# Spreading the inverse norms of the differential heads: transposes on TensorE or two transfers through DRAM

## The chip, the cores and the metric

The kernel runs on one core of one Trainium2 chip. A core has five engines with instruction queues of their own: TensorE (PE; its weight loads are listed as PEld), VectorE (DVE), ScalarE (ACT), GpSimd (POOL) and SyncE (SP), which here only issues transfers. Each engine works through its queue in order, and waits at an instruction until the semaphores that it names are reached. 16 DMA engines carry out the transfers. Matmul results go to PSUM banks; everything else lies in SBUF, 128 partitions wide, or in DRAM.

The metric is device time of one execution in microseconds (us). Before the change it was 1777.44 us, the median of three runs from 1776.35 to 1777.76.

## The reference

Two layers over 512 tokens of width 1024. Each layer mixes tokens in three branches (differential attention, a convolution module, neighbourhood attention), merges them by gates, and goes on to a feed-forward block and a gated embedding. What concerns this change is the end of the differential attention:

```python
def diff_attention(qa, ka, va, lq1, lk1, lq2, lk2, subln_g, lam_init, cos, sin):
    ...
    def block(qi):
        s = jnp.einsum('bhcqd,bhckd->bhcqk', qi, k).astype(f32) * scale
        a = jax.nn.softmax(s, axis=-1)
        a = (a[:, :, 0] - lam * a[:, :, 1]).astype(v.dtype)
        return jnp.einsum('bhqk,bhkd->bhqd', a, v)
    o = lax.map(block, qb)
    o = o.transpose(1, 2, 0, 3, 4).reshape(B, HA, S, DV_A)
    o = rmsnorm(o, subln_g) * (1.0 - lam_init)
    return o.transpose(0, 2, 1, 3).reshape(B, S, WIDTH_A)
```

There are four heads of 128 value channels. For each head and token the norm needs one number, the inverse root of the mean square over the 128 channels.

## The kernel before

**Layout.** Activations stand with channels on partitions and the 512 tokens along the free dimension, so a head's output `o` is one tile of 128 x 512. Its norm sums over partitions. All products are done in three passes on split operands (`split`, line 162: ACT makes the high part, DVE subtracts it for the low part; `mm3`, line 175: three matmuls). Weights come by SP into three raw buffers `wr` (`weights`, line 166), are split into three buffers `wh` and `wl`, and are used by TensorE some tiles later. When a raw buffer is split, the next load may go into it.

**Order.** The order on TensorE is written by hand. Work that runs beside the projections is a generator: after every four chunks of three matmuls `tick` (line 94) advances the generators whose delay has run out; a `yield n` puts the next part n ticks later. For the other engines a scheduler places instructions by priority and by what they need; `behind` (line 1064) adds that one instruction may not go before another, without a wait. On SP the order of transfers is fixed in the same way, and a transfer that waits holds all that stand behind it.

**The head's norm.** `diff_unit` (line 844) makes scores and probabilities of a quarter of the queries (`probs`, line 892), transposes the probabilities and multiplies them by the values. When a head's output is complete in the bank `av`, ACT writes its squares to `sq` (tag `ss`, one buffer) and a scaled copy to `o` (tag `t`). Then `norm` (line 206) runs:

1. After 1 tick, four transposes of `sq` into a PSUM bank `tr` (line 213), tokens now on partitions.
2. DVE sums over the free dimension and adds epsilon (lines 216 to 221), which gives `ms`, 128 x 4: token 128c + p in row p, column c.
3. POOL raises it to the power -0.5, which gives the column `col` (tag `rc`, line 223).
4. After 2 ticks, four more transposes (line 227). Each takes one column of `col`, repeated 128 times, and so puts the inverse norms of 128 tokens as a row on all 128 partitions. They fill a bank `bc` of 128 x 512.
5. `done` (line 884): DVE multiplies `o` by `bc`, read from PSUM, ACT and DVE split it into a tile `y`, which the merge of the branches (`merge_a`, line 776) multiplies much later.

`norm` has other users too (the norms over the model width, the convolution's norm). They pass `spread=True` and copy `bc` to SBUF first. Only the differential heads pass `spread=False`.

While the heads' norms run, TensorE goes on with projections: the third and fourth heads' query and key (`diff_in`, line 813), the gates (`gate_c`, `gate_b`), the product of the third branch (`branch_c`, line 769). `diff_in` sends four copies of 32 rows over SP for each rotation (`diff_rp`, line 829) and stacks the halves by more copies (line 660). DVE fills its time with taps of the convolution (`conv_z`).

Of the kernel before, what the change touches and what calls it, by code (L numbers as in the profile page):

```python
# [11 lines left out]
F32 = mybir.dt.float32  # L12
# [3 lines left out]
ALU = mybir.AluOpType  # L16
# [4 lines left out]
P = 128  # L21
L = 2
S = 512
# [4 lines left out]
HA = 4  # L28
# [33 lines left out]
class Net:  # L62
# [143 lines left out]
    def norm(self, sq, n, waits, done, spread=True, eps=None):  # L206


        nc = self.nc
        yield waits[0]  # L210
        st = self.ps("tr", (P, 4, P))
        for c in range(4):
            nc.tensor.transpose(st[:, c, :], sq[:, c * P:(c + 1) * P], self.ident)
        with self.tc.high_priority(offset=min(200, self.tc.cur_priority - self.p0) if n == D and self.p0 is not None else 0):
            sm = self.sb("sm", [P, 4])
            nc.vector.tensor_reduce(out=sm, in_=st, op=ALU.add, axis=AX.X)
            ms = self.sb("sm", [P, 4])
            if eps is None:
                nc.vector.tensor_scalar(ms, sm, 1.0 / n, EPS, ALU.mult, ALU.add)
            else:  # L220
                self.stt(ms, sm, 1.0 / n, eps, ALU.mult, ALU.add)
            col = self.sb("rc", [P, 4])
            nc.gpsimd.tensor_tensor(col, ms, self.power, ALU.pow)
        yield waits[1]
        bc = self.ps("tr", (P, 4, P))
        for c in range(4):
            nc.tensor.transpose(bc[:, c, :], col[:, c:c + 1].to_broadcast([P, P]), self.ident)
        bc = bc.rearrange("p a b -> p (a b)")
        done(col, self.spread(bc) if spread else bc)

    def rows(self, col, rb):
        self.col, self.rb = col, rb
# [59 lines left out]
    def build(self):  # L292
        nc, tc, a = self.nc, self.tc, self.a
        self.bufs = dict(wr=3, wh=3, wl=3, h=8, qk=2, kh=2, v=4, pt=2, y=5, z=5, x=4, t=7, rp=4,
                         e=4, a=3, r=2, rb=1, ss=1, sm=8, rc=4, b=2, s=8)
        self.bg, self.w_ahead = BG, 400
        self.pbufs = dict(mm=3, sc=2, tr=2, av=1)
        with tc.tile_pool(name="sb", bufs=1) as self.pool, \
                tc.tile_pool(name="ps", bufs=1, space=PSUM) as self.psum, \
                tc.tile_pool(name="dr", bufs=1, space=DRAM) as dram:  # L300
            xs = dram.tile([KD, P, 512], F32, name="xs")
            self.pis = dram.tile([KD, P, 512], F32, name="pis")
            with tc.manual_schedule(engines={mybir.EngineType.PE}):
                h = self.opening()
                xsrc = a["xT"]
                for i in range(L):
                    h = self.layer(i, h, xsrc, xs)
                    xsrc = xs
# [535 lines left out]
    def diff_unit(self, head, qt, st4, k2, st, box, ys):  # L844

        nc, i = self.nc, self.i
        half, t = qt // 2, qt % 2
        box[qt] = self.probs(st4, k2, qt, box["s0"])
        if t == 0:
            return  # L850
        yield 3
        ats = [box[2 * half], box[2 * half + 1]]
        pps = []
        for kp in range(2):
            pt = self.ps("tr", (P, 2, 256))
            for u in range(2):
                for t in range(2):
                    kc = 2 * kp + u
                    nc.tensor.transpose(pt[:, u, t * P:(t + 1) * P],
                                        ats[t][:, kc * P:(kc + 1) * P], self.ident)  # L860
            pp = self.sb("pt", [P, 2, 2, 256], F32R)
            self.split(pp[:, 0], pp[:, 1], pt)
            pps.append(pp)
        yield 2
        if half == 0:
            box["av"] = self.ps("av")
        av = box["av"]
        cs = slice((head % 2) * P, (head % 2) * P + P)
        for kp in range(2):
            for u in range(2):  # L870
                v = st["v", head // 2][kp][:, u].rearrange("p (a b) -> p a b", a=2)
                self.mm3(av[:, half * 256:half * 256 + 256], v[:, 0, cs], v[:, 1, cs],
                         pps[kp][:, 0, u], pps[kp][:, 1, u], kp * 2 + u == 0, kp * 2 + u == 3)
        if half == 0:
            return

        eps = self.sb("sm", [P, 4])
        self.stt(eps, box["s0"], EPS, box["s0"], ALU.mult, ALU.mult)
        o = self.sb("t", [P, 512])
        sq = self.sb("ss", [P, 512])  # L880
        self.act(sq, av, AF.Square)
        self.act(o, av, AF.Copy, scale=self.subg[:, i:i + 1])

        def done(col, bc):
            self.tt(o, o, bc, ALU.mult)
            y = self.sb("y", [P, 2, 512], F32R)
            self.split(y[:, 0, :], y[:, 1, :], o)
            ys.append(y)

        yield from self.norm(sq, P, (1, 2), done, spread=False, eps=eps)  # L890

    def probs(self, st4, k2, qt, s0):


        nc, i = self.nc, self.i
        qs = slice(qt * P, (qt + 1) * P)
        m = self.sb("s", [P, 10])
        es = []
        for u in range(2):
            sc = self.ps("sc")  # L900
            self.scores(sc, st4, k2, u, qs, slice(0, 512))
            nc.vector.tensor_reduce(out=m[:, u:u + 1], in_=sc, op=ALU.max, axis=AX.X, negate=True)  # L902
            e = self.sb("e" if u else "a", [P, 512])
            self.act(e, sc, AF.Exp, table="exp", bias=m[:, u:u + 1],
                     accum_out=m[:, 3:4] if u else s0[:, qt:qt + 1])
            es.append(e)
        nc.vector.reciprocal(m[:, 4:5], m[:, 3:4])
        self.stt(m[:, 5:6], m[:, 4:5], self.nlam[:, i:i + 1], s0[:, qt:qt + 1],
                 ALU.mult, ALU.mult)
        self.stt(es[0], es[1], m[:, 5:6], es[0], ALU.mult, ALU.add)  # L910
        return es[0]

    def w_o(self, mg, xsrc):
# [553 lines left out]
```

## Time and profile before

| | us |
|---|---|
| median of three runs | 1777.44 |
| lowest and highest run | 1776.35, 1777.76 |
| profiled execution, first to last instruction (its span) | 1776.7 |
| DVE busy in the span | 1421.7 |
| line 227, differential heads: 32 transposes, length of one | 0.272 |
| line 213, differential heads: 32 transposes, length of one | 0.272 |
| line 223, differential heads: 8 powers on POOL, length of one | 1.0 to 1.5 |

For the profiled execution only the span is listed. Its matmuls overlap: the next starts before the last has ended, so what a matmul costs is read from the distance of starts, not from its length. A row of the timeline gives start, length, engine, line, operation, tiles written and read, shape, and in brackets the idle time of the engine before it with what ended it. Line 157 and 160 are helpers of DVE, line 143 one of ACT; such rows are told apart by their tiles. SPq is SP's queue: the length of its row is the time from one transfer's start of issue to the end of issue, waits between merged ones included.

### The profile page before, as it was taken

What the parts mean: (1) busy time and instruction counts of PE and PEld (TensorE: products, weight loads), DVE (VectorE), ACT (ScalarE), POOL (GpSimd) and SP (SyncE); (2) the same over time, 40 slices, a digit from 0 to 9 for tenths busy, and PEclk for the clock granted to TensorE, in tenths of its full rate; (3) what the DMA queues carried; (4) which work ended last, traced back from release to release, by engine and by line L of the source; (5) the groups of instructions that cost most, each with busy time, mean ns of one, the idle gap of its engine ahead of it and who ended that gap; (6) DMA issues with size and microseconds to landing.
All of it is one profiled execution on the core that took longest, in us unless ns stands there. A gap on an engine that the chain in (4) does not pass through costs nothing.

```text
span 1776.7 us, 27451 instructions
## 1 busy us (share of the span) xinstructions
PE 1767.5 (99%) x10210; PEld 1559.6 (88%) x10210; DVE 1421.7 (80%) x2418; ACT 894.4 (50%) x1561; POOL 103.0 (6%) x146
## 2 busy tenths in 40 slices
PE   9999999999999999999999999999999999999998
PEld 7888888888899899998888888888888998989987
DVE  7878887998798587787776788889887976867776
ACT  5577555225565254454545765452356643534454
POOL 0000000000111010100000000000001110101000
PEclk9999999999999999999999999999999999999999
DMA  5666641334757366543447655423357664655332
GB/s 202 188 186 176 161 125 42 113 98 140 230 150 193 109 167 160 132 131 123 145 124 198 176 165 149 113 71 95 93 179 198 171 179 115 173 144 151 98 108 92
DMA packets 113509, 256.07 MB, mean 144 GB/s; under 512 B 14560, under 2 KB 19424, under 8 KB 113376
## 3 DMA queue, kind: packets, MB, share of 16 engines
q1 hardware_dynamic: 99984, 229.93, 42.3%
q0 software_dynamic: 12672, 23.07, 8.3%
q8 instruction: 81, 1.33, 0.3%
q10 hardware_dynamic: 720, 1.31, 0.2%
q14 instruction: 52, 0.43, 0.1%
HBM read 215.46 MB, written 7.34 MB: 125 GB/s over the span
## 4 chain that ended last, share of the span: by engine, by line
PE 96%; DVE 2%; ACT 1%; issue 0%; DMA 0%; POOL 0%; ACTq 0%; POOLq 0%; DVEq 0%
PE ffn_mm L1017 4%; PE ffn_mm L1019 4%; PE ffn_mm L177 4%; PE ffn_mm L179 4%; PE ffn_mm L178 4%; PE ffn_mm L1018 4%; PE ffn_sc L1019 3%; PE ffn_sc L1017 3%; PE ffn_sc L1018 3%; PE mergea_mm L177 2%; PE mergea_mm L178 2%; PE mergea_mm L179 2%; PE diff_sc L811 2%; PE gatec_mm L177 2%; PE gatec_mm L178 2%; PE gatec_mm L179 2%
## 5 line engine op out<-in xcount | busy, mean ns | idle before, releaser
L160 DVE SCALAR_TENSOR_TENSOR conv_z<-glu_z,pre_par,conv_z 128x512 f32<-128x512 f32 x240 | 179.4, 748 | 3.3
L143 ACT ACTIVATE ffn_wh<-ffn_wr 128x1024 fp32r<-128x1024 f32 (+1 forms) x92 | 92.7, 1014 | 111.7 <-PE ffn_mm L178 77.1
L987 POOL DMA_DIRECT2D ffn_qk<-w_fu x88 | 78.0, 990 | 605.7 <-DMA ffn_qk<-w_fu 414.7
L157 DVE TENSOR_TENSOR ffn_wl<-ffn_wr,ffn_wh 128x1024 fp32r<-128x1024 f32 (+1 forms) x92 | 107.4, 1173 | 5.4 <-ACT ffn_wh L143 4.9
L157 DVE TENSOR_TENSOR ffn_t<-ffn_mm,wo_rb 128x512 f32<-128x512 f32 (+1 forms) x64 | 38.6, 604 | 67.9 <-PE ffn_mm L179 67.8
L143 ACT ACTIVATE mergea_wh<-mergea_wr 128x1024 fp32r<-128x1024 f32 (+1 forms) x32 | 27.1, 846 | 96.8 <-PE mergea_mm L178 79.6
L143 ACT ACTIVATE ffn_wh<-ffn_qk 128x1024 fp32r<-128x1024 f32 x44 | 46.7, 1060 | 35.9 <-PE ffn_mm L178 15.7
L157 DVE TENSOR_TENSOR ffn_wl<-ffn_qk,ffn_wh 128x1024 fp32r<-128x1024 f32 x44 | 53.8, 1224 | 11.3 <-ACT ffn_wh L143 11.3
L157 DVE TENSOR_TENSOR ffn_t<-ffn_t,ffn_t 128x512 f32<-128x512 f32 (+1 forms) x46 | 31.3, 680 | 31.4 <-ACT ffn_t L143 30.9
L143 ACT ACTIVATE diff_a<-diff_sc,diff_s 128x512 f32<-128x512 f32 x32 | 22.0, 686 | 61.0 <-DVE diff_s L902 61.0
L177 PE MATMUL ffn_mm<-ffn_v,ffn_wh 128*128 128x512 f32 x132 | 51.4, 389 | 0.0
L178 PE MATMUL ffn_mm<-ffn_v,ffn_wh 128*128 128x512 f32 x132 | 51.4, 389 | 0.0
L179 PE MATMUL ffn_mm<-ffn_v,ffn_wl 128*128 128x512 f32 x132 | 51.3, 389 | 0.0
L177 PE MATMUL ffn_mm<-ffn_y,ffn_wh 128*128 128x512 f32 x132 | 51.3, 389 | 0.0
L178 PE MATMUL ffn_mm<-ffn_y,ffn_wh 128*128 128x512 f32 x132 | 51.3, 389 | 0.0
L179 PE MATMUL ffn_mm<-ffn_y,ffn_wl 128*128 128x512 f32 x132 | 51.3, 389 | 0.0
L1019 PE MATMUL ffn_mm<-wo_h,ffn_wl 128*128 128x256 f32 x176 | 49.8, 283 | 0.0
L1019 PE MATMUL ffn_sc<-wo_h,ffn_wl 128*128 128x256 f32 x176 | 49.8, 283 | 0.0
L1018 PE MATMUL ffn_mm<-wo_h,ffn_wh 128*128 128x256 f32 x176 | 49.8, 283 | 0.0
L1018 PE MATMUL ffn_sc<-wo_h,ffn_wh 128*128 128x256 f32 x176 | 49.8, 283 | 0.0
L1017 PE MATMUL ffn_sc<-wo_h,ffn_wh 128*128 128x256 f32 x176 | 49.8, 283 | 0.0
L1017 PE MATMUL ffn_mm<-wo_h,ffn_wh 128*128 128x256 f32 x176 | 49.8, 283 | 0.0
(876 smaller groups left out, 6588.6 us busy)
## 6 DMA issues: line engine op xcount, KB each, us to landing
ffn_qk<-w_fu POOLq DMA_DIRECT2D x88, 256.0 KB, 5.7
ffn_wr<-w_fg SPq DMA_DIRECT2D x44, 512.0 KB, 3.7
ffn_wr<-w_fd SPq DMA_DIRECT2D x32, 448.0 KB, 3.9
ffn_r<-w_fu SPq DMA_DIRECT2D x44, 256.0 KB, 3.7
ffn_qk<-w_fg SPq DMA_DIRECT2D x44, 256.0 KB, 4.3
ffn_qk<-w_fu SPq DMA_DIRECT2D x44, 256.0 KB, 4.6
natten_wr<-w_in SPq DMA_DIRECT2D x16, 512.0 KB, 4.3
natten_b<-bias SPq DMA_DIRECT2D x32, 256.0 KB, 4.0
```

The source lines that it names most:

```text
L143: i = self.nc.scalar.activation(out, in_, func, **kw)
L157: return self.nc.vector.tensor_tensor(out, a, b, op)
L160: return self.nc.vector.scalar_tensor_tensor(out, a, s, b, op0, op1)
L177: mm(out, wh, ah, start=first, stop=False)
L178: mm(out, wh, al, start=False, stop=False)
L179: mm(out, wl, ah, start=False, stop=last)
L811: self.nc.tensor.matmul(out, st4[:, u, qs], st[:, ks], start=n == 0, stop=n == 1)
L987: nc.gpsimd.dma_start(q, wu[:, lo], accum_op=ALU.add)
L1017: mm(out, wh[:, c], bh, start=first and k == 0, stop=False, skip_group_check=True)
L1018: mm(out, wh[:, c], bl, start=False, stop=False, skip_group_check=True)
L1019: mm(out, wl[:, c], bh, start=False, stop=k == 3, skip_group_check=True)
```

## The change

For the differential heads the second four transposes are gone. SP writes the 128 x 4 column to a row of 512 numbers in DRAM, element by element, and reads this row back on all 128 partitions, into the buffer of the squares. The multiplication reads SBUF where it read PSUM; it is placed four ticks after the statistics, where it was two, and it may go ahead neither of the latest weight split nor of the latest part of the probabilities.

```diff
@@ norm
             col = self.sb("rc", [P, 4])
             nc.gpsimd.tensor_tensor(col, ms, self.power, ALU.pow)
+        if not spread:
+            rows, self.rowed = self.nrm[self.rowed], self.rowed + 1
+            with nc.allow_non_contiguous_dma(reason="column to row"):
+                nc.sync.dma_start(rows.rearrange("(c p) -> p c", p=P), col)
+            nc.sync.dma_start(sq, rows[None, :].to_broadcast([P, S]))
+            yield sum(waits[1:])
+            return done(col, sq)
         yield waits[1]
...
-        done(col, self.spread(bc) if spread else bc)
+        done(col, self.spread(bc))
@@ build
+            self.nrm, self.rowed = dram.tile([L * HA, S], F32, name="nrm"), 0
@@ diff_unit
-            self.split(pp[:, 0], pp[:, 1], pt)
+            self.prob = self.split(pp[:, 0], pp[:, 1], pt)
...
         def done(col, bc):
-            self.tt(o, o, bc, ALU.mult)
+            i = self.tt(o, o, bc, ALU.mult)
+            self.behind(i, self.low)
+            self.behind(i, self.prob)
...
-        yield from self.norm(sq, P, (1, 2), done, spread=False, eps=eps)
+        yield from self.norm(sq, P, (1, 4), done, spread=False, eps=eps)
@@ probs
-        self.stt(es[0], es[1], m[:, 5:6], es[0], ALU.mult, ALU.add)
+        self.prob = self.stt(es[0], es[1], m[:, 5:6], es[0], ALU.mult, ALU.add)
```

In the changed program TensorE has the same order without the eight groups of four transposes, and POOL's order is unchanged. On SP the two transfers of head 0 stand between two loads of weights for the gates; those of head 1 before a load for the second gates; those of head 2 after the third load of the third branch's weights; those of head 3 around the last load for the second gates, the write before it and the read after it. On DVE the multiplication of heads 0, 1 and 2 stands right behind the mix of the next probabilities, that of head 3 between the low parts of the last two gate weights; some taps of the convolution and the splits of the head outputs have moved. On ACT the load of the sigmoid table and two of its uses stand a little earlier.

## The prediction

> **What bounds the kernel now.** I began with the page: span, busy shares, and the chain of work that ended last.
>
> ```profile
> span 1776.7 us, 27451 instructions
> PE 1767.5 (99%) x10210; PEld 1559.6 (88%) x10210; DVE 1421.7 (80%) x2418; ACT 894.4 (50%) x1561; POOL 103.0 (6%) x146
> PE 96%; DVE 2%; ACT 1%; issue 0%; DMA 0%; POOL 0%; ACTq 0%; POOLq 0%; DVEq 0%
> ```
>
> TensorE carries 96% of the chain. A busy share of 99% is not proof, since matmul records overlap, so next came the view of waits for PE alone (waits, times, longest) and the busy time by stretch in the stage that the change touches (differential heads, layer 0).
>
> ```profile
> PE pre_av L325 <- DVE pre_zeror L398: 1.1, 1, 1.1
> PE natten_tr L734 <- ACT natten_e L143: 0.3, 2, 0.2
> PE natten_tr L736 <- ACT natten_e L143: 0.3, 2, 0.2
> PE natten_tr L736 <- DVE natten_a L157: 0.2, 1, 0.2
> ...
> 217.00:320.00 103.00, 103.00 (x529) 86.99 (x528) 85.88 (x148) 52.74 (x103) 4.53 (x4) 1.00 0.34 97
> ```
>
> All waits of PE add up to 1.9 us, and none is in the touched stage, where PE is busy for 103.00 of 103.00 us at full granted clock. DVE is next with 85.88 us; the DMA engines are at 0.34. So here a TensorE instruction removed is time removed, and an instruction of another engine costs only when it is late enough to stop TensorE.
>
> The Trainium skill ("Perfetto Trace Analysis", section Identifying the Most-Contended Engine) says that matmul busy time measures headroom badly, because matmuls are pipelined, and that the busy share of weight loads is better. By that rule PE is 88% and not 99% full here, and removed PE work might win nothing; this is rival C, and the starts of the matmuls below decide it.
>
> **The price of the removed transposes.** The line's own group, then PE in order of time (start, length) around head 0, and further down a place with the same neighbours and no transposes.
>
> ```profile
> L227 PE MATMUL diff_tr<-pre_ident,diff_rc x32: 270/272/273, 224.9 to 1194.4; 128*128 128x128 f32 x32
> ...
> 224.65 0.39 PE L179 MATMUL diff_mm<-glu_h,diff_wl 128*128 128x512 f32 x1
> 224.88 0.60 PE L227 MATMUL diff_tr<-pre_ident,diff_rc 128*128 128x128 f32 x4
> 225.23 0.47 PE L811 MATMUL diff_sc<-diff_qk 128*128 128x512 f32 x1
> ...
> 226.24 0.39 PE L177 MATMUL diff_mm<-glu_h,diff_wh 128*128 128x512 f32 x1
> ...
> 227.85 0.39 PE L178 MATMUL diff_mm<-glu_h,diff_wh 128*128 128x512 f32 x1
> ...
> 232.94 0.39 PE L179 MATMUL gatec_mm<-glu_h,gatec_wl 128*128 128x512 f32 x1
> ...
> 234.07 0.39 PE L177 MATMUL gatec_mm<-glu_h,gatec_wh 128*128 128x512 f32 x1
> ```
>
> 32 transposes are 8 groups of four (4 heads, 2 layers). Lengths overlap, so I count starts. From a weight product over four score products to the next weight product takes 234.07 - 232.94 = 1.13 us undisturbed, five steps of 0.226 us. With the group between it takes 226.24 - 224.65 = 1.59 us: 0.46 us more. Over twelve steps it is 227.85 - 224.65 = 3.20 us against 12 x 0.226 = 2.71: 0.49 us, as the products just after a group still start a little late. I take 0.47, between the two, and 8 x 0.47 = 3.8 us. The ends: the four starts alone (225.23 - 224.88 = 0.35, 2.8 us in all) and the group's whole length (0.60, 4.8 us in all). By these starts PE has no slack beneath its busy share.
>
> **What is added: two transfers on SP's queue per head.** In the changed program's order, SP first waits for the column from POOL, writes it to DRAM one 4-byte element at a time (512 of them), waits for that to land, and reads it back as 128 rows of 2 KB (256 KB). POOL gives the column here (heads 0 and 3 of layer 0):
>
> ```profile
> 219.16 1.02 POOL L223 TENSOR_TENSOR diff_rc<-diff_sm,pre_power 128x4 f32<-128x4 f32 x1 [55.51 <-DVE diff_sm L160]
> ...
> 311.75 1.50 POOL L223 TENSOR_TENSOR diff_rc<-diff_sm,pre_power 128x4 f32<-128x4 f32 x1 [29.29 <-DVE diff_sm L160]
> ```
>
> So the column is there at 220.18 and 313.25. No 4-byte write stands in the trace. Nearest rows (issues: count, KB each, us to landing; and the queue's packets with their share of 16 engines' time):
>
> ```profile
> q1 hardware_dynamic: 99984, 229.93, 42.3%
> ...
> gatec_wr<-w_in SPq DMA_DIRECT2D x16, 512.0 KB, 4.0
> ...
> diff_rp<-diff_rp SPq DMA_DIRECT2D x64, 64.0 KB, 3.5
> ...
> branchc_wr<-w_br_c SPq DMA_DIRECT2D x16, 256.0 KB, 2.7
> ...
> pis<-pin_t SPq DMA_DIRECT2D x12, 256.0 KB, 2.1
> ple_a<-pis SPq DMA_DIRECT2D x12, 256.0 KB, 3.1
> ...
> wo_x<-xs SPq DMA_DIRECT2D x8, 256.0 KB, 7.0
> ```
>
> A packet costs 0.423 x 16 x 1776.7 / 99984 = 0.120 us of one engine. The write: from below, a store of 128 rows to DRAM, 2.1 us (8 packets on each engine). 512 packets are 32 on each, 24 more: 24 x 0.120 = 2.9, so 5.0 us. From above 2.1 + 32 x 0.120 = 5.9. I take 5.0, since a small packet is cheaper in bytes but not shown cheaper in time. The read: from below 2.7, from above 7.0 (a crowded stage); I take 3.1, the same kind of read in a stage about as busy. Two issues with their waits, 0.4 us each (a load's issue holds SP 0.33 us, the first row of the next fence). The pair: 0.8 + 5.0 + 3.1 = 8.9 us; the ends 5.6 and 13.7.
>
> **What waits behind it, head 0.** Behind the waiting write stand, on SP, the read, one weight load and the five rotation copies; behind the multiplication, on DVE, stand the next weight split, the rotary products and the maxima of the next scores. SP, DVE, ACT and PE before:
>
> ```profile
> 316.07 0.33 SPq L171 DMA_DIRECT2D mergea_wr<-w_in  x1
> ...
> 200.52 2.41 SPq L829 DMA_DIRECT2D diff_rp<-diff_rp  x4
> ...
> 218.21 5.73 SPq L171 DMA_DIRECT2D gatec_wr<-w_in  x2
> 224.03 7.00 SPq L829 DMA_DIRECT2D diff_rp<-diff_rp  x5
> ...
> 225.51 0.69 DVE L157 TENSOR_TENSOR diff_t<-diff_t,diff_tr 128x512 f32<-128x512 f32 x1 [0.74 <-PE diff_tr L227]
> ...
> 228.77 0.75 DVE L160 SCALAR_TENSOR_TENSOR diff_a<-diff_e,diff_s,diff_a 128x512 f32<-128x512 f32 x1
> 230.05 1.23 DVE L157 TENSOR_TENSOR gatec_wl<-gatec_wr,gatec_wh 128x1024 fp32r<-128x1024 f32 x1 [0.53 <-ACT gatec_wh L143]
> 231.19 0.68 DVE L157 TENSOR_TENSOR diff_rp<-diff_rp,diff_r 128x512 f32<-128x512 f32 x1
> ...
> 235.23 0.68 DVE L902 TENSOR_REDUCE diff_s<-diff_sc 128x1 f32<-128x512 f32 x1
> ...
> 235.94 0.69 ACT L143 ACTIVATE diff_e<-diff_sc,diff_s 128x512 f32<-128x512 f32 x1 [0.62 <-DVE diff_s L902]
> ...
> 244.02 1.04 ACT L143 ACTIVATE gatec_wh<-gatec_wr 128x1024 fp32r<-128x1024 f32 x1
> ...
> 240.40 0.39 PE L811 MATMUL diff_sc<-diff_qk 128*128 128x512 f32 x1
> ```
>
> The multiplication itself costs nothing new: 0.69 us from PSUM, 0.68 for a product of two SBUF tiles of that shape. It moves from 225.51 to behind the mix that ends at 229.52. The pair lands at 220.2 + 8.9 = 229.1: just in time. What is late if it is late: the second maximum (ends 235.91), the exponential that empties the score bank (ends 236.63), then the scores that take the bank at 240.40. Spare: 240.40 - 236.63 = 3.8 us. The multiplication and the split of its result come in front, but a split of the rotary result goes behind the maxima, so they keep their time. So the pair may take 229.5 + 3.8 - 220.2 = 13.1 us, against 13.7 at the upper end.
>
> The copies start when the read is issued: 220.2 + 0.4 + 5.0 + 0.4 = 226.0, the weight load goes out by 226.4, the last of four copies (2.41 us for four) at 228.2, and lands after 3.5 us at 231.7. DVE's rotary product, now at about 231.4, waits 0.3 us of the same 3.8. That allows a write of 5.0 + 3.8 - 0.3 = 8.5 us. The weight load, before at 223.94 - 0.33 = 223.6, goes out near 226.4 and lands after 4.0 near 230.4. With three raw buffers its split is the one at 244.02: 13 us of cover.
>
> **Head 3 and the others.** The multiplication stands between these two on DVE, and PE needs the second's result at the third product of the next gate:
>
> ```profile
> 320.31 0.74 DVE L160 SCALAR_TENSOR_TENSOR conv_z<-glu_z,pre_par,conv_z 128x512 f32<-128x512 f32 x1
> ...
> 321.57 1.22 DVE L157 TENSOR_TENSOR gateb_wl<-gateb_wr,gateb_wh 128x1024 fp32r<-128x1024 f32 x1
> ...
> 329.04 0.39 PE L179 MATMUL gateb_mm<-glu_h,gateb_wl 128*128 128x512 f32 x1
> ```
>
> The pair lands at 313.3 + 8.9 = 322.2, so DVE is held 1.1 us at 321.05; it could be held to 329.04 - 1.22 - 0.69 = 327.1, a pair of 13.9 us. Heads 1 and 2 have only weight loads behind their transfers. The reordered convolution taps, the earlier table load and the transpose bank that is free sooner are no work more or less, and PE waits for none of them. The 2.1 MB of added reads meet DMA engines at 0.34.
>
> **Sum.** -8 x 0.47 = -3.8, transfers and waits 0. On the profiled span: 1776.7 - 3.8 = 1772.9 us. The median of the runs stands 0.7 above that span, which I take as what lies around it: 1777.44 - 3.8 = **1773.7 us**. Bounds: 4.8 saved gives 1772.6; at the upper end the pair passes head 0's limit by 0.6 us, once in each layer, and 2.8 - 1.2 = 1.6 saved gives 1775.8.
>
> **Rivals.** *A, the gain partly eaten* by a late read that holds DVE at head 0: 1775.8, as just worked out. For it: the landing is forecast only 0.4 us before its slot. Against it: 3.8 us of cover come after.
>
> *B, slower: the scatter write.* If its 512 elements drain one after the other on one engine instead of over 16, it takes 512 x 0.120 = 61 us. It decides from a write of 8.5 us. Each head would then hold SP, with it copies and weights, for 61 - 8.5 = 53 us that PE lacks; about 8 x 53 = 420 us, or some 2200 us. For it: nothing in the trace is written in such pieces. Against it: every other transfer of 128 partitions lands in 2 to 7 us, so is spread. The Trainium skill ("DMA: Bandwidth & Descriptors", Rules for kernel authors) warns that a strided last dimension becomes one descriptor per element, and that a transposing plain copy is 19 times slower than the hardware transpose; 19 x 2.1 us would be an estimate of 40 us for the write and, by the same holding, some 250 us more in all. No row here shows either.
>
> *C, the change does not do what it says:* the transposes leave, but the time stays, because PE was not full there or a later stage is paced by other engines. For it: DVE and ACT have 3% of the chain. Against it: the 0.46 us more between the same neighbours, and PE's waits of 1.9 us in all, which leave little to be paced by. Time 1777.4.
>
> **How the numbers follow.** Forecast 0.66, A 0.14, C 0.08, B 0.12. A measurement of this kernel can tell about 0.2% (3.55 us, below 1773.9) from no change, and 3.8 us is 0.21%: the forecast lies on that edge. I give it 0.55 for faster and 0.11 for within; A adds 0.03 to faster and 0.11 to within; C 0.08 to within; B 0.12 to slower. Faster 0.58, within 0.30, slower 0.12. Range 1772.4 to 1776.2: the forecast and A with the bounds above and 0.2 to 0.4 us of run scatter; B and C, 0.20, are left out.
>
> **What would show it.** Right: no L227 group of the heads on PE; score products following weight products at 0.226 us at those places; the chain still 96% PE; a write near 5 us and a read near 3 us; DVE idle before the multiplication by a DMA for at most about 1 us. A shows as a PE wait before L811 scores on ACT or DVE some 20 us after head 0's statistics. B shows as a write over 8.5 us and PE waiting for copies and weights. Wrong altogether: a PE wait that is new elsewhere, or a span shorter by much less than 3.8 with none.

## The result, and the profile after

| | before | after |
|---|---|---|
| median of five runs, us | 1777.44 | 1808.89 |
| lowest and highest, us | 1775.95, 1777.76 | 1808.38, 1812.02 |
| span of the profiled execution, us | 1776.7 | 1807.1 |

The change makes the kernel slower: ratio 1.0186, 95% interval 1.0173 to 1.0198. The forecast was 1773.7 us. The page after the change begins so:

```profile
span 1807.1 us, 27420 instructions
...
PE 1773.0 (98%) x10178; PEld 1559.3 (86%) x10178; DVE 1420.6 (79%) x2418; ACT 892.8 (49%) x1561; POOL 103.2 (6%) x146
```

The 32 transposes are gone from TensorE (10210 - 32 = 10178 matmuls), and yet the span has grown by 30.4 us. So TensorE must stand still somewhere. The view of its waits (in total, times, longest) names four new lines, all from the stage of the differential heads and the gates:

```profile
PE gateb_mm L177 <- DVE gatec_x L157: 17.0, 2, 8.7
PE diff_sc L819 <- ACT diff_a L143: 4.2, 4, 2.7
PE diff_tr L213 <- ACT diff_ss L143: 3.6, 4, 0.9
PE diff_av L178 <- DVE diff_pt L157: 1.7, 3, 1.3
PE pre_av L333 <- DVE pre_zeror L406: 1.1, 1, 1.1
```

They add up to 26.5 us; the last line was there before. Added up by starts instead (each start of a matmul that comes over 0.12 us later after the one before it than such a pair usually does), the stage holds 30.2 us of pauses and 4.0 us of slow steps right behind them: 34.2 us, of which the removed transposes give 3.8 back. That accounts for the 30.4.

The largest wait falls at head 3, once per layer. SP's, ACT's, DVE's and PE's timelines there, in layer 0 (start, length, and in brackets the idle time before with what ended it):

```profile
321.26 0.38 SPq L227 DMA_DIRECT2D nrm<-diff_rc  x1
321.77 0.42 SPq L171 DMA_DIRECT2D gateb_wr<-w_in  x1
330.86 0.33 SPq L228 DMA_DIRECT2D diff_ss<-nrm  x1
```

```profile
334.81 1.06 ACT L143 ACTIVATE gateb_wh<-gateb_wr 128x1024 fp32r<-128x1024 f32 x1 [11.35 <-DMA gateb_wr<-w_in]
```

```profile
336.31 0.69 DVE L157 TENSOR_TENSOR diff_t<-diff_t,diff_ss 128x512 f32<-128x512 f32 x1 [7.79 <-DMA diff_ss<-nrm]
336.92 1.22 DVE L157 TENSOR_TENSOR gateb_wl<-gateb_wr,gateb_wh 128x1024 fp32r<-128x1024 f32 x1
338.05 1.89 DVE L157 TENSOR_TENSOR diff_y<-diff_t,diff_y 128x512 fp32r<-128x512 f32 x3
339.86 1.22 DVE L157 TENSOR_TENSOR mergea_wl<-mergea_wr,mergea_wh 128x1024 fp32r<-128x1024 f32 x1
341.00 0.68 DVE L157 TENSOR_TENSOR gatec_x<-gatec_x,branchc_mm 128x512 f32<-128x512 f32 x1
```

```profile
333.07 0.39 PE L179 MATMUL gateb_mm<-glu_h,gateb_wl 128*128 128x512 f32 x1
341.82 0.77 PE L177 MATMUL gateb_mm<-glu_h,gateb_wh 128*128 128x512 f32 x1 [8.37 <-DVE gatec_x L157]
342.38 0.63 PE L178 MATMUL gateb_mm<-glu_h,gateb_wh 128*128 128x512 f32 x1
342.81 0.63 PE L179 MATMUL gateb_mm<-glu_h,gateb_wl 128*128 128x512 f32 x1
...
345.11 0.39 PE L179 MATMUL gateb_mm<-glu_h,gateb_wl 128*128 128x512 f32 x1
345.34 0.40 PE L177 MATMUL gateb_mm<-glu_h,gateb_wh 128*128 128x512 f32 x1
```

Read them from the end. TensorE stops after 333.07 because the next gate product needs the bank of the third branch, which DVE empties with the addition into `gatec_x`. This addition ends at 341.68 and stands 341.68 - 336.31 = 5.4 us behind the multiplication, which has waited 7.79 us for the rows. The read was issued at 330.86, 9.6 us after the write, because SP waits for the write's landing in between. And a 512 KB weight load that slipped out between the two, at 321.77, ends ACT's wait only at 334.8. The issues of the whole run (KB each, median us to landing), and the moving of the packets from 322 to 324 us, in 40 slices of 0.05 us, and from 328 to 330:

```profile
diff_ss<-nrm SPq DMA_DIRECT2D x8, 256.0 KB, 4.4
...
nrm<-diff_rc SPq DMA_DIRECT2D x8, 2.0 KB, 9.9
```

```profile
DMA  0001797787200000000000000900000000000093
...
DMA packets 536, 0.03 MB, mean 17 GB/s; under 512 B 528, under 2 KB 528, under 8 KB 536
```

```profile
DMA packets 12, 0.05 MB, mean 25 GB/s; under 512 B 0, under 2 KB 0, under 8 KB 12
```

The 512 elements pass the engines in about 0.4 us (322.15 to 322.55). Then next to nothing moves for 8 us: 12 packets of the weight load in 2 us. The engines are not idle in this lull. The load's packets start, and stay; from 324 to 326 us:

```profile
DMA packets 21, 0.09 MB, mean 43 GB/s; under 512 B 0, under 2 KB 0, under 8 KB 21
...
q1 hardware_dynamic: 21, 0.09, 233.2%
```

The last number is the time that these 21 packets took, as a share of what 16 engines have in the 2 us: 3.6 us for each on average. In the kernel before, no packet takes over 1.9 us; here some take over 9. The write counts as landed at 330.8, and the load's packets flow again only some 2.5 us later (11 packets start from 331 to 333 us, 147 from 333 to 335). Over the eight heads the write lands after 7.3 to 11.2 us.

### The profile page after: what moved, and what is told of

Same layout as the page of the kernel before. It is cut to its first block, busy times and chain, and to the rows that moved or that the text cites. A ratio compares the mean times of both kernels' runs of the same rounds, so it can differ in the third digit from the quotient of the medians.

```text
span 1807.1 us, 27420 instructions
## 1 busy us (share of the span) xinstructions
PE 1773.0 (98%) x10178; PEld 1559.3 (86%) x10178; DVE 1420.6 (79%) x2418; ACT 892.8 (49%) x1561; POOL 103.2 (6%) x146
## 5 line engine op out<-in xcount | busy, mean ns | idle before, releaser
L157 DVE TENSOR_TENSOR ffn_wl<-ffn_qk,ffn_wh 128x1024 fp32r<-128x1024 f32 x44 | 53.9, 1224 | 10.7 <-ACT ffn_wh L143 10.7
```

What stands on the lines that cost most here:

```text
L157: return self.nc.vector.tensor_tensor(out, a, b, op)
```

## The experiments

The first four kernels separate order, queue and write pattern. "Theory" in the expectations is as stated there. Medians are set against the runs of the kernel before on the same chip (1776.6 to 1777.2 us).

**Order alone.** The two transfers leave; the rules for the place of the multiplication stay as the change has them.

```diff
-            with nc.allow_non_contiguous_dma(reason="column to row"):
-                nc.sync.dma_start(rows.rearrange("(c p) -> p c", p=P), col)
-            nc.sync.dma_start(sq, rows[None, :].to_broadcast([P, S]))
             yield sum(waits[1:])
```

> The changed kernel without its two transfers: the multiplication takes the squares that already lie in SBUF, so the inverse norm is left out of the product; the eight groups of four transposes stay away and the multiplication keeps its later place by the same rules. Theory (the write's late landing is the whole loss): all of 8 x 0.47 = 3.8 us is gained, 1773.7 us, between 1772.6 and 1774.6, and PE has no new wait. Rival (the moved instructions on DVE and ACT alone keep the matmul bank of the next gate): 1790 us or more, with PE's wait at L177 gateb_mm on DVE gatec_x still there.

Measured: 1772.99 us against 1776.61, ratio 0.9979 [0.9970, 0.9989]. The transposes are worth 3.6 us. But this kernel does not hold the change's order at head 3. With no transfer to wait for, the multiplication starts there at 312.1 us, ahead of both low parts of the gate weights, and the addition that frees the bank at 319.1, ahead of the second low part. In the mended kernel below, whose order is the change's, these come at 318.9 and 324.0. Head 3 has such a new order in every kernel below that does not read the rows there. That the new places of instructions cost nothing by themselves is shown by the mended kernel, not by this one.

**Queue alone.** The transfers run, but the read goes to a spare tile and nobody waits for it.

```diff
-            nc.sync.dma_start(sq, rows[None, :].to_broadcast([P, S]))
+            nc.sync.dma_start(self.gap, rows[None, :GAP].to_broadcast([P, GAP]))
...
```

> As the run without transfers, but SP again writes the column to DRAM in 512 elements and, after its landing, reads 144 of the numbers back into a spare tile that nobody uses; the multiplication does not wait for it and the inverse norm is left out of the product. It has SP's hold and whatever the write does to the transfers behind it, not DVE's hold. Theory A (DVE held by the multiplication is the loss): 1773 to 1778 us, the write still lands after 7 to 11 us. Theory B (the loads queued behind the write are late): the load of the last gate weight lands 10 us or later after its issue and PE waits some 8 us at L177 gateb_mm in each layer; 1790 to 1800 us.

Measured: 1785.67 us, ratio 1.0051 [1.0035, 1.0067]. This lies between the two ranges, and 12.7 us over the first kernel, with VectorE never held by the rows. The write lands after 7.9 to 11.6 us here too, and the last gate weights 12.4 to 12.6 us after their issue, but PE does not wait for them as Theory B said; with head 3's order changed, they are not needed so soon. Counted product by product (each matmul's start against that of the same matmul in the mended kernel below), 10.2 us are lost at head 0 of the two layers: SP holds the rotation copies until the write has landed, and PE waits for scores (3.0 us) and then for probabilities (3.0).

**Another queue.** Both transfers are issued by GpSimd.

```diff
-                nc.sync.dma_start(rows.rearrange("(c p) -> p c", p=P), col)
-            nc.sync.dma_start(sq, rows[None, :].to_broadcast([P, S]))
+                nc.gpsimd.dma_start(rows.rearrange("(c p) -> p c", p=P), col)
+            nc.gpsimd.dma_start(sq, rows[None, :].to_broadcast([P, S]))
```

> The changed kernel with both transfers issued by POOL on its own queue; DVE still waits for the read, SP waits for nothing new. Theory A (DVE's hold): the time stays at 1795 us or more, as long as the write lands after 7 us or more. Theory B (SP's hold and the transfers queued behind the write on its queue): loads on SP land after 3 to 5 us as before and the time falls to 1774 to 1785 us. If the write lands quickly from POOL's queue (under 4 us) both give about 1774, and the write's slowness belongs to SP's queue.

Measured: 1819.61 us, ratio 1.0241 [1.0221, 1.0262], slower than the change itself. SP no longer waits, but the write takes 9.4 to 10.7 us all the same, and VectorE is held for the rows as in the change (10.9 us at head 3, where its order is another again). The largest wait of PE, some 10 us once per layer, stands one group of gate products earlier than in the change, and the split of the head's output, which its view names, follows the multiplication too:

```profile
PE gateb_mm L177 <- ACT diff_y L143: 20.1, 2, 10.3
```

At head 3 of layer 0 the write is issued at 324.4, and a weight load from SP's own queue, 2.3 us later, has this landing (view of its tile in that stretch):

```profile
L171 SPq DMA_DIRECT2D mergea_wr<-w_in x1: 327/327/327, 326.7 to 326.7; - x1
...
DMA to landing us min/median/max: 11.6/11.6/11.6
```

A load of this size otherwise lands in 3.5 us. So it is not the order of a queue that stops the loads: they crawl beside the 4-byte writes, whether these stand in their queue or in another.

**Write patterns.** Unread as above, each head with another pattern: 128 runs of 16 bytes (head 0), 512 elements 512 bytes apart (head 1), 256 elements side by side (head 2), 512 side by side as in the change (head 3).

```diff
+                if head == 0:
+                    nc.sync.dma_start(rows.rearrange("(p c) -> p c", c=4), col)
+                elif head == 1:
+                    nc.sync.dma_start(self.far.rearrange("(c p) o -> p c o", p=P)[:, :, 0], col)
+                elif head == 2:
+                    nc.sync.dma_start(rows[0:256].rearrange("(c p) -> p c", p=P), col[:, 0:2])
...
```

> As the run with transfers that nobody reads, with another write pattern for each head, the inverse norm left out of the product: head 0 writes 128 runs of 16 bytes to neighbouring places, head 1 writes 512 elements of 4 bytes that lie 512 bytes apart, head 2 writes 256 elements of 4 bytes, head 3 the 512 dense elements of the changed kernel. In the changed kernel the writes of heads 0 to 3 land after 7.3, 10.0, 11.2 and 9.5 us in layer 0. If every write costs in proportion to its count of elements: head 0 about 2 to 3.5 us, head 1 about 10, head 2 about 5.5, head 3 as before. If elements that share one short stretch of DRAM hinder each other: head 1 falls to 3 to 5 us while head 0 stays above 5. If the landing of any write to DRAM is simply late there: all four near 7 to 11.

The view of each write line (heads 0 to 3 in turn) gives the landings, two per pattern:

```profile
L229 SPq DMA_DIRECT2D nrm<-diff_rc x2: 332/334/337, 219.3 to 1098.6; - x2
...
DMA to landing us min/median/max: 1.9/1.9/1.9
```

```profile
L231 SPq DMA_DIRECT2D far<-diff_rc x2: 391/391/391, 250.0 to 1129.4; - x2
...
DMA to landing us min/median/max: 1.8/2.0/2.2
```

```profile
DMA to landing us min/median/max: 7.9/9.0/10.2
```

```profile
DMA to landing us min/median/max: 9.5/10.6/11.7
```

512 elements of 4 bytes land in 2.0 us when they lie far apart; half as many side by side take 9.0. So the count of elements is not the price, and a write to DRAM is not late as such. The forecast by neighbours is met in head 1 and missed in head 0: its runs of 16 bytes lie side by side too, and land in 1.9 us. What is late is elements of 4 bytes side by side. The whole, one run, took 1774.37 us; since two heads had quick patterns, the time by itself tells little.

**Spacing.** The same, with 8, 16, 32 and 64 bytes from element to element in heads 0 to 3.

```diff
+            self.fars = [dram.tile([S, w], F32, name=f"far{4 * w}") for w in (2, 4, 8, 16)]
...
+                nc.sync.dma_start(far.rearrange("(c p) o -> p c o", p=P)[:, :, 0], col)
...
```

> Transfers unread as in e2_transfers_unread (the multiplication takes the squares, the inverse norm is left out); 512 writes of 4 bytes, spaced 8 bytes in head 0, 16 in head 1, 32 in head 2 and 64 in head 3; 128 numbers are read back. Theory 1 (neighbours in one short stretch of DRAM finish one after another): landing falls with the spacing, 7 to 10 us at 8 bytes to 2 us at 64. Rival (it is the whole 2 KB that matters, one tensor's packets over one place): still 5 us or more at 32, where 512 writes cover 16 KB.

Landings in layers 0 and 1: 4.2 and 3.6 us at 8 bytes, 2.5 and 2.7 at 16, 2.0 and 2.0 at 32, 2.3 and 3.1 at 64; one run, 1773.01 us. At 8 bytes this is less than the 7 to 10 us of the theory. Most of the lateness is gone from 16 bytes on, and the runs of 16 bytes above start 16 bytes apart as well: in all these rows a write is late where elements start less than 16 bytes apart. The rival, which still had 5 us at 32 bytes, falls.

**The write mended.** Partition p writes its four numbers as one run of 16 bytes; the multiplication takes the rows in that order.

```diff
-            with nc.allow_non_contiguous_dma(reason="column to row"):
-                nc.sync.dma_start(rows.rearrange("(c p) -> p c", p=P), col)
+            nc.sync.dma_start(rows.rearrange("(p c) -> p c", c=4), col)
...
-            return done(col, sq)
+            return done(col, sq.rearrange("q (p c) -> q c p", c=4))
...
-            i = self.tt(o, o, bc, ALU.mult)
+            ov = o.rearrange("q (c p) -> q c p", c=4)
+            i = self.tt(ov, ov, bc, ALU.mult)
```

> The write puts each partition's four numbers side by side in DRAM (128 runs of 16 bytes in place of 512 of 4); the read is unchanged, and the multiplication takes the rows through a strided view. All four heads of both layers in full. Theory 1 (the 4-byte neighbours land late, and every loss follows from that landing): the write lands in 1.9 us as in head 0 of e4_patterns, the pair in 1.9 + 4.5 + two issues = 7 us; at head 3 the multiplication came up in the changed kernel 7.2 us after the write's issue (321.3 to 328.5), so it does not wait; no wait of the multiplication of the bank behind gatec_x; 1773.0 to 1774.5 us, as e1_no_transfers within 1.5. Rival (a wait on any transfer costs the queue and VectorE, and the strided multiplication is dear): over 1780 us with waits of 1 to 3 us left at each head.

Measured: 1772.89 us against 1776.79, ratio 0.9978 [0.9969, 0.9987], faster than both kernels and equal to the kernel without transfers. SP, VectorE, ScalarE and GpSimd have the change's instructions in the change's order; only the pattern of the write and the view in the multiplication differ. The write lands after 1.4 to 2.2 us, and no multiplication waits, though it takes longer through the strided view, 1.09 us instead of 0.69 (the view of the write's line, and the multiplication's line in the view of `diff_t`):

```profile
DMA to landing us min/median/max: 1.4/1.4/2.2
```

```profile
L157 DVE TENSOR_TENSOR diff_t<-diff_t,diff_ss x8: 1079/1091/1104, 228.7 to 1196.7; 128x512 f32<-128x512 f32 x8
```

**Three heads only.** The mended write in heads 0 to 2, and head 3 by transposes as before the change (the condition becomes `if not spread and self.rowed % HA < HA - 1`).

> Runs of 16 bytes in heads 0 to 2, head 3 by transposes on TensorE and a multiplication out of PSUM as in the kernel before. Theory 1: 1773.0 + 2 x 0.47 = 1773.9 to 1775 us, slower than f1_runs16 by 0.5 to 1 unless that still waits at head 3. Rival (head 3 is where any transfer costs): faster than f1_runs16.

Measured: 1774.16 us, ratio 0.9985 [0.9975, 0.9994], 1.3 us over the kernel with all four heads; two groups of transposes were priced at 0.9. With a quick write, head 3 is no worse a place for a transfer than the others.

**Head 3 unread.** The change's own write; heads 0 to 2 in full, head 3 reads into the spare tile.

```diff
+            last = self.rowed % HA == 0
...
+            if last:
+                nc.sync.dma_start(self.gap, rows[None, :GAP].to_broadcast([P, GAP]))
+            else:
+                nc.sync.dma_start(sq, rows[None, :].to_broadcast([P, S]))
...
```

> The changed kernel with its 4-byte writes, but head 3 of each layer reads 144 numbers into a spare tile and multiplies by the squares, which lie in the SBUF already (its inverse norm is left out); heads 0 to 2 in full. Theory 1 (of the loss, the part over e2_transfers_unread is VectorE held at head 3, before gatec_x): 1785.7 + at most 3 = 1785 to 1789 us, with no wait of gateb_mm for gatec_x. Rival (VectorE held at each of the heads costs alike): a quarter of the 23 us between the two goes, 1802 to 1804 us.

Measured: 1797.94 us, ratio 1.0119 [1.0101, 1.0138]. Neither figure was met: the wait of the multiplication at head 3, together with the change's order there, is worth 11 of the change's 36 us over the kernel without transfers, more than a quarter of the 23 us but less than half. PE's waits show why:

```profile
PE diff_sc L823 <- ACT diff_a L143: 5.2, 4, 3.6
PE gateb_mm L177 <- ACT gateb_wh L143: 4.1, 2, 2.3
PE diff_tr L213 <- ACT diff_ss L143: 3.5, 4, 0.9
```

No wait of `gateb_mm` for `gatec_x` is left, but the crawling weight load takes its place: the gate product now waits for `gateb_wh`. In the change, two late things ended within 2 us of each other, and removing one uncovers the other.

**Late, but by quick transfers.** The mended kernel, with the numbers going twice more to DRAM and back before the last write.

```diff
+            for src, row, dst in ((col, r1, g[:, 0:4]), (g[:, 0:4], r2, g[:, 4:8])):
+                nc.sync.dma_start(row.rearrange("(p c) -> p c", c=4), src)
+                nc.sync.dma_start(dst, row.rearrange("(p c) -> p c", c=4))
-            nc.sync.dma_start(rows.rearrange("(p c) -> p c", c=4), col)
+            nc.sync.dma_start(rows.rearrange("(p c) -> p c", c=4), g[:, 4:8])
...
```

> As f1_runs16, but the numbers go twice more to DRAM and back on SyncE's queue before the write (five quick transfers of 128 runs of 16 bytes, each waiting for the one before: 3 x 1.4 us of writes as measured in f1_runs16, 2 reads at some 1.6, issues between them), so that the rows lie in DRAM some 9 us after the first issue, as with the 4-byte writes, with nothing of 4 bytes in flight. Theory A (lateness alone: the queue and VectorE held): most of the loss comes back, 1800 to 1808 us, with gatec_x holding the matmul bank at head 3. Theory B (the other loads, which crawl beside the 4-byte writes, make most of it): under 1790 us. Loads behind take their usual 3.6 to 5 us in both.

Measured: 1773.31 us, ratio 0.9979 [0.9970, 0.9989], which seems to speak against lateness as the cause. It doesn't: the scheduler knew of the four more transfers, put other transfers of SP between them, and moved the multiplication. DVE's timeline at head 3:

```profile
325.61 0.69 DVE L157 TENSOR_TENSOR gatec_x<-gatec_x,branchc_mm 128x512 f32<-128x512 f32 x1
...
329.26 1.07 DVE L157 TENSOR_TENSOR diff_t<-diff_t,diff_ss 128x512 f32<-128x512 f32 x1 [2.30 <-DMA diff_ss<-nrm]
```

The addition that frees the bank now goes first. The rows came 16 us after the first issue (313.0 to 329.2), later than in the change, and cost nothing, because nothing that TensorE needed soon stood behind them.

**Neighbours beside.** The mended kernel, and the change's 4-byte write to a row that nobody reads.

```diff
+            with nc.allow_non_contiguous_dma(reason="column to row"):
+                nc.sync.dma_start(self.dense[self.rowed - 1].rearrange("(c p) -> p c", p=P), col)
...
```

> As f1_runs16 (16-byte runs, rows read and used), and behind the read the 512 writes of 4 bytes of the changed kernel go to another row that nobody reads: nothing waits for them, neither SyncE nor VectorE. Theory A (lateness alone): within 1 us of f1_runs16, 1772.9 to 1774 us, or a few us if a load crawls behind them (gateb_wr to 11 us and more). Theory B (the crawl of other loads makes most of it): over 1785 us, with waits of ScalarE for gateb_wr of some 8 us.

Measured: 1826.78 us, ratio 1.0279 [1.0264, 1.0295], the slowest of all. But it does not show what it was made for: the scheduler issued the spare write ahead of the read, and the read crawled with the rest.

```profile
diff_ss<-nrm SPq DMA_DIRECT2D x8, 256.0 KB, 13.3
...
dense<-diff_rc SPq DMA_DIRECT2D x8, 2.0 KB, 11.3
```

Neither kernel had told lateness from crawl, so two cleaner ones were made, whose instructions on SP and VectorE stand in the mended kernel's order (the second has one issue more per head).

**Lateness alone.** Seven more powers on GpSimd go into the tile that the read fills, so that the read waits for them.

```diff
+            for c in range(7):
+                nc.gpsimd.tensor_tensor(sq[:, 4 * c:4 * c + 4], ms, self.power, ALU.pow)
             nc.sync.dma_start(sq, rows[None, :].to_broadcast([P, S]))
```

> As f1_runs16 (16-byte runs, rows read and used), with seven more powers of 128x4 on GpSimd (1.5 us each in the changed kernel), written into the tile that the read fills, so that the read waits for them on SyncE's queue some 9 to 10 us after the write, as it waits for the landing in the changed kernel. The instructions on SyncE and VectorE stand in the order of the changed kernel, one by one, which was not so in f6_late_quick, where the multiplication of head 3 was moved behind gatec_x; nothing of 4 bytes is in flight. Theory A (lateness alone: queue and VectorE held): 1798 to 1808 us, with gateb_mm waiting for gatec_x some 4 to 8 us at head 3. Theory B (the crawl of other transfers is most of it): 1773 to 1786 us.

Measured: 1788.37 us, ratio 1.0066 [1.0051, 1.0081], between the two ranges. GpSimd took two of the seven before the column's own power, so the write came some 2 us later and the read 5.0 to 6.3 us after it: less late than in the change, where it was 7.4 to 11.3. The powers did not slow VectorE, whose instructions beside them took as long as in the mended kernel. SP's timeline, DVE's and the waits of PE:

```profile
316.36 0.33 SPq L226 DMA_DIRECT2D nrm<-diff_rc  x1
...
322.65 0.33 SPq L229 DMA_DIRECT2D diff_ss<-nrm  x1
```

```profile
327.07 1.06 DVE L157 TENSOR_TENSOR diff_t<-diff_t,diff_ss 128x512 f32<-128x512 f32 x1 [5.62 <-DMA diff_ss<-nrm]
```

```profile
PE gateb_mm L177 <- DVE gatec_x L157: 7.5, 2, 3.8
```

The wait for `gatec_x` is back, with no 4-byte write anywhere and every load of the gates landing within 5.6 us. With the change's order, this smaller lateness cost 15.5 us over the mended kernel.

**Crawl alone.** The mended kernel, and after each multiplication the 4-byte write from the multiplied tile, so that it delays neither the read nor the multiplication.

```diff
+                self.nc.sync.dma_start(self.dense[self.rowed - 1].rearrange("(c p) -> p c", p=P), o[:, 0:4])
...
```

> As f1_runs16, and after each multiplication 512 writes of 4 bytes go to another row of DRAM, which nobody reads, from the multiplied tile: they can delay neither the read (as they did in f7_dense_beside, where they went out ahead of it) nor the multiplication, and no instruction waits for their landing. Order on VectorE and ScalarE as in f1_runs16, SyncE's with one issue more per head. Theory A (lateness alone): 1773 to 1775 us. Theory B (transfers behind crawl until the 4-byte writes have landed): rotation copies and weights behind them land up to 10 us late, PE waits for diff_sc and for mergea's weights, 1782 to 1810 us.

Measured: 1789.34 us, ratio 1.0069 [1.0052, 1.0086], 16.4 us over the mended kernel, in the range of Theory B, though PE waits at another product than it named. Nobody waits for this write; what loses time are the rotation copies behind it at head 0 (waits of DVE, then of PE):

```profile
DVE diff_rp L157 <- DMA diff_rp<-diff_rp: 16.3, 3, 8.2
```

```profile
PE diff_av L178 <- DVE diff_pt L157: 10.9, 2, 5.6
```

It is not that SP was held: in layer 0 these transfers are issued within 0.5 us of their times in the mended kernel. The issues from 230.2 to 233.2 us (last number: us to landing), in the mended kernel and here:

```profile
gatec_wr<-w_in SPq DMA_DIRECT2D x1, 512.0 KB, 3.9
diff_rp<-diff_rp SPq DMA_DIRECT2D x4, 64.0 KB, 3.3
```

```profile
gatec_wr<-w_in SPq DMA_DIRECT2D x1, 512.0 KB, 13.4
diff_rp<-diff_rp SPq DMA_DIRECT2D x4, 64.0 KB, 12.7
```

The copies go from SBUF to SBUF and touch no DRAM, and they crawl all the same.

## Why the prediction was wrong, by its steps

- *The price of the transposes, 3.8 us.* Right: 3.6 us without transfers, 3.9 with the mended write. Rival C falls with it; TensorE was as full as the distance of its starts said.
- *The reordering costs nothing.* Right by itself: the mended kernel, with the change's order on SP, VectorE, ScalarE and GpSimd, saves the full amount. But the same order is what makes a late read dear.
- *The write, 5.0 us, at most 5.9.* **This is the step that failed.** It measured 7.3 to 11.2, median 9.9. The sum took 32 packets on each engine at the mean time of a packet. The packets did pass quickly, 0.4 us for all; what takes the time comes after the last packet and hangs on elements that start less than 16 bytes apart, for which no row of the trace before stood. So the upper bound had no row under it.
- *The read, 3.1 us (2.7 to 7.0).* 3.2 to 5.6, inside its bounds. The pair at head 3 took 15.0 us from the write's issue (321.3) to the multiplication (336.3), where 8.9 was forecast and 13.7 the end.
- *Head 0, spare of 13.1 us for the pair and 8.5 for the write.* The mechanism was right: PE waits for scores there, 0.9 us in layer 0 and 2.7 in layer 1, where A had looked for it; the waits for probabilities (`diff_av`) and for squares (`diff_tr`) behind them were not named. The limits were too wide: in layer 0 the write took 7.3 us and the pair 13.0 (220.4 to 233.4), both inside them, and yet TensorE fell 4.5 us behind the mended kernel from there to the next head's squares.
- *Head 3, spare of 13.9 us.* Wrong independently of the landing. Only the second low part of the gate weights was named as queued behind the multiplication. The addition into `gatec_x`, 5.4 us behind it, frees the bank for the next gate product. TensorE needed that bank at 333.3, so the multiplication had to start at 327.9, which is 6.6 us after the write, and not 13.9. It started at 336.3, 8.4 us late, and TensorE waited 8.37. In the mended kernel, where no earlier head is late, the same count gives some 9 us: the write is issued at 311.5, the addition ends 5.8 us after the multiplication's start, and the product comes at 326.55.
- *Loads behind the transfers have cover.* So it was argued for head 0, and for heads 1 and 2 only weight loads were named. At head 3, `gateb_wr` crawled for 12.9 us instead of 3.6; that is hidden in the change behind the wait for `gatec_x`, and appears as soon as this is taken away.
- *Rival B* had the right side, but its point (a write over 8.5 us) was too high by the head 0 above, and its mechanism and size were wrong: 512 packets that pass in 0.4 us do not drain over one engine, and no write takes 61 us. The page of the Trainium skill cited there ("DMA: Bandwidth & Descriptors", Rules for kernel authors) counts descriptors, one per element; 512 of them land in 2.0 us when spaced by 32 or 512 bytes, so the count is not what costs here. The same page of the Trainium skill, in its section Anatomy of one DMA, which is on transfers issued by GpSimd, says that a transfer's semaphore waits until the last byte is confirmed in the target memory, for most of some 2 us. The stretch between the last packet and the landing is what grew here, to 8.2 us at head 3 with SP issuing (322.55 to 330.8); issued by GpSimd, the whole write took 9.4 to 10.7.

Two things stay open. Why neighbouring 4-byte writes are confirmed so late, and why the packets of other transfers stick beside them, is not visible in a trace. The Trainium skill ("DMA: Bandwidth & Descriptors", Specifications) says that transfers under 512 bytes are done by reading, changing and writing back. That would fit writes that meet in one place, but no run here shows that step, and by itself it does not tell the late writes from the runs of 16 bytes and the spaced elements, which are under 512 bytes too and land in 1.4 to 3.1 us.

And the 36 us between the change and the mended kernel split by place, not by cause. TensorE's order is the same in both; product by product, the change falls behind by 6.5 and 8.2 us at heads 0 to 2 of the two layers, and by 10.0 and 11.1 at head 3. Lateness alone, smaller than the change's, cost 15.5, most of it at head 0 and head 3. The 16.4 of crawl alone are no share of the 36: they arose from copies that the change issues only after the write has landed. In the change one weight load per layer, at head 3, is issued beside the write, and what it adds to the wait for the rows there is not separated.

## What to carry to other kernels

A column that must become a row in DRAM is written in the order in which the partitions hold it, as one run per partition, and the shuffle is done by a strided view where the data are used: that alone turned 1.9% slower into 0.2% faster. When a transfer is put in the place of engine work, price the transfer by a row of the same pattern of addresses or call its upper end unknown, and list everything that stands behind the waiting instruction on its engine up to the first thing that TensorE needs, bank releases included. The order in front of a late landing is part of the cost: where the scheduler knew of four more transfers, it put the release first, and rows that came 16 us after the first issue cost nothing. What landing time it had counted on in the change is not on record.

## What the runs showed of the hardware that was not expected

- **Landing of 512 elements of 4 bytes in DRAM, by spacing:** 7.3 to 11.2 us side by side in the change, 3.6 to 4.2 at 8 bytes, 2.5 to 2.7 at 16, 2.0 at 32, 2.3 to 3.1 at 64, 1.8 to 2.2 at 512. As 128 runs of 16 bytes, side by side, 1.4 to 2.2.
- **Other transfers crawl meanwhile, in the write's queue or in another:** 512 KB loads issued within 3.1 us after such a write land after 11.0 to 14.3 us over all runs, where none takes over 4.9 in the kernel before; a 256 KB read behind a spare write after 13.3 instead of 4.4 (medians); copies of 64 KB within SBUF after 12.7 instead of 3.3.
- **TensorE comes back slowly from a pause.** After 8.4 us of standing still its products start 0.43 us apart for some 2.5 us (from 342.38 above) before the usual 0.23 returns. The same follows the wait of 2.7 us in layer 1 (granted clock 0.83 from 1134 to 1144 us), and not the waits of 0.9 and 1.3 us in layer 0 (1.00 from 240 to 250). The stretches of the changed kernel from 332.5 to 342 and from 342 to 352 us show it in the clock, the third number from the right:

```profile
332.50:342.00 9.50, 1.13 (x6) 0.66 (x5) 5.69 (x8) 4.79 (x7) 0.00 (x0) 0.79 0.64 189
342.00:352.00 10.00, 10.00 (x39) 8.13 (x40) 9.79 (x15) 1.54 (x2) 0.00 (x0) 0.86 0.26 80
```
